# Short products held back into groups in a two-layer DeltaNet and attention trunk

## The chip, the cores and the metric

The kernel runs on one core of a Trainium2 chip. The metric is device time in microseconds (us) of one execution. The engines are TensorE (PE, with PEld for its weight loads), VectorE (DVE), ScalarE (ACT), GpSimd (POOL) and SyncE (SP), which issues the DMAs here. A line such as L137 is a line of the kernel before; the change adds lines, so that the same helper stands at L142 in the changed kernel.

## The reference, cut to what matters

Two layers over 1024 tokens of width 1024: a gated DeltaNet with chunked recurrence, then an attention with forget gates. Each is `x + gate * mixer(norm(x))`. The change concerns the first layer:

```python
def gated_delta_rule(q, k, v, g, beta):          # 16 value heads, head size 128
    ...
    L = jnp.where(strict, jnp.einsum('bhncd,bhnsd->bhncs', kb, k) * decay, 0.0)
    T = lax.linalg.triangular_solve(eye + L, ...)     # the inverse
    u = T @ vb
    w = T @ (kb * jnp.exp(g)[..., None])
    ...
    def step(state, inp):                             # the recurrence
        v_new = u_n - jnp.einsum('bhcd,bhde->bhce', w_n, state)
        o = (jnp.einsum('bhcd,bhde->bhce', q_n, state)
             + jnp.einsum('bhcs,bhse->bhce', a_n, v_new))
        state = state * gl_n[..., None, None] + jnp.einsum('bhcd,bhce->bhde', k_n, v_new)
        return state, o
```

Around it stand the input projection with a short causal convolution, and `o = rmsnorm(o, norm_w) * zg` followed by the output projection.

## The kernel before

The first layer is worked off in 16 iterations: two halves of 512 tokens, and in each half 8 groups of two value heads. The kernel uses chunks of 128 tokens, four in a half. Per iteration there are:

- the input projections (`proj_all`, `proj_tile`): long products with 512 columns, each weight and activation split in a high and a low part, so that three products stand for one (tiles `mm<-ht_h,whi`, `ht_l,whi`, `ht_h,wlo`). After the last iteration, `out_proj_a` adds the output projection of the first half (`mm<-whi,ohi` and its like) while the last recurrences still run, and later that of the second half, whose activations are loaded in pairs of heads (tiles `yh`, `yl`, L461);
- transposes and small products of preparation (`prepk`, `prepv`, `prep2`; tiles `tr`, `su`);
- the inverse of the triangular matrix, by blocks of 16, 32 and 64 (`invert_blocks` on VectorE and DMAs, `invert_merge` with products of 16, 32 and 64 columns; tiles `tmat`, `rmat`, `qq`, `pp`, `pq`);
- the recurrence (`chain`, L1033): per chunk `ch<-state,k` (the state read), VectorE's `xp` (L1050), `ch<-xp,rmat`, ScalarE's `vn` and VectorE's `ve`, `co<-vn`, `co<-ve`, VectorE's new `state` (L1095), and so on to the next chunk;
- `finish` (L1117): the output `og` is normalised, transposed (`tr<-ident,og`), gated, split in `ogh` and `ogl` (one buffer each) and stored to `og_d` and `ogl_d` (L1142), from which the output projection loads it again.

The long products are float32r, the short ones float32; a short product therefore shows as two records in the trace, a transpose as one.

The order of TensorE's instructions is written out by hand through a planner, the class `Flow`. Each of the streams above is a generator. `flow.t` is a plan clock that adds up the planned cost of each product. A generator yields a delay after which its next piece may be issued; `step` takes, among the streams that are due, the one with the lowest priority number. The long products are the stream with number 9, the fill; recurrence, inverse, preparation and finish have the numbers 1 to 6. So before the change a short piece is issued in the first step after it is due, and the fill takes what is left, three products at a time. Streams also hold on each other: `done["core"]` counts finished chains, and the projections of an iteration wait until an earlier chain is done. The order of the other engines and of SyncE's queue is made by the scheduler from this program, so a piece that moves takes its DMAs and vector instructions along.

Of the kernel before, what the change touches and what calls it, by code (L numbers as in the profile page):

```python
# [78 lines left out]
SC = 1.0  # L79
OGW = 2000  # L80
OL = 4
OX = 4
Y_NN = 8000
KPE = (7, 5)
KC = 3
# [26 lines left out]
class Flow:  # L112


    def __init__(self, tc):
        self.tc = tc
        self.nc = tc.nc
        self.t = 0.0
        self.n = 0
        self.live = []  # L120
        self.idle = 0.0
        self.rings = {}
        self.held = []
        self.kept = ()

    def _cost(self, lhs, rhs):
        n = rhs.free_size()
        if lhs.dtype == BF16:
            return max(0.42 * n, 29.0)
        m = lhs.free_size()  # L130
        if lhs.dtype == F32R:
            return max(0.42 * n, 107.0 * m / P)
        return max(1.67 * n, 214.0 * m / P)
# [43 lines left out]
            self.step()  # L177

    def step(self):
        for s in self.live:  # L180
            if s[3] <= self.t:
                with self.tc.high_priority(offset=s[4]):
                    d = next(s[2], None)
                if d is None:
                    self.live.remove(s)
                else:
                    s[3] = self.t + d * SC
                break
        else:
            t = min(s[3] for s in self.live)  # L190
            self.idle += t - self.t
            self.t = t
# [3 lines left out]
def tile_trunk(  # L196
# [26 lines left out]
    flow = Flow(tc)  # L223
# [127 lines left out]
    def hold(ok):  # L351
        while not ok():
            yield 300
# [90 lines left out]
    def out_o(k, tok):  # L444
        def load():
            w = 2 * P
            hi = xt_([P, w], "ohi", 4, F32R)
            lo = xt_([P, w], "olo", 4, F32R)
            for v, d in ((hi, og_d), (lo, ogl_d)):
                nc.sync.dma_start(v.bitcast(F32), d[k, :, tok : tok + w])  # L450
            return [(hi, lo)]

        return load
# [13 lines left out]
    def out_list(h):  # L467
        n = (512, D)[h]
        for tp in range(0, CPH, 2):
            for cs in range(0, D, n):  # L470
                w_src.extend(out_w(k, cs, n) for k in range(0, 16, D // n))
                if h:
                    k0 = 0 if tp else OX
                    o_src.extend(out_o(k, h * HALF + tp * P) for k in range(k0))
# [56 lines left out]
    with ExitStack() as sa:  # L531
# [3 lines left out]
        def at(shape, name, bufs=1, dt=F32):  # L535
            return pa.tile(shape, dt, name=name, tag=name, bufs=bufs)
# [128 lines left out]
        def norm_tile(xt, jk, evac, part=None):  # L665
# [4 lines left out]
            nc.vector.tensor_scalar(xt, xt, rs, None, op0=ALU.mult)  # L670
            yield Y_NN
            for k0 in range(0, KT, 4):
# [603 lines left out]
        def ada_all():  # L1276
            yield from hold(lambda: done["kp"] >= AD0 + 1)
            def al(shape, name, bufs):
                t = at([P, D], name, bufs) if name == "nx" else at([P, 512], name, bufs)
                return t[0 : shape[0], 0 : shape[1]]  # L1280

            for _ in range(2):
                nc.vector.tensor_copy(al([P, KT], "nx", 2), ts[AD0]["k"][:, 0, 0:KT])
            for l, cl in strips:
                yield from ada_strip(
                    al, acc_bank, l, cl, 512, ("nx", 2), ("nh", 2), ("nh", 2), 1, ADP
                )

        ts = []
        done = dict(kp=0, prep2=0, merge=0, kqv=0, tr=0, prep=0, chain=0, norm=0, start=0, inv=0, core=0, gates=0)  # L1290
# [11 lines left out]
        flow.add(prep2_all(), 4, HP)  # L1302
        flow.add(next_norm(), 5)
        flow.add(ada_all(), 6)
        flow.run(ch)
        while done["chain"] < 2 * NG:
            flow.step()
# [636 lines left out]
```

## Time and profile before

| | us |
|---|---|
| median of 3 runs | 1946.24 (1943.46 to 1947.99) |
| profiled execution | 1945.78 |
| its span, first to last instruction | 1943.8 |
| mean granted TensorE clock | 0.971 |

Stages by the trace: the start to about 165 us, iterations of the first layer to about 1051 us, the output projection's first half to about 1079 us and its second half from there to about 1200 us, then the second layer. The end of the third chain is near 321 us, that of the thirteenth near 884 us.

In the rows below, a timeline row has start and duration in us, then the engine, the line, the operation, the tiles (out<-in) and shapes and a count; in brackets the idle time of the engine before it and what ended that. A row of waits has total, times and longest, in us.

### The profile page before, as it was taken

The page shows a single profiled execution, that of the slowest core. Times are in us where ns is not written, and L with a number is a line of the kernel's source. Part 1 is how long each engine was busy: PE and PEld are TensorE (multiplying, and loading weights), DVE is VectorE, ACT ScalarE, POOL GpSimd, SP SyncE. Part 2 cuts the span into 40 slices and gives each one's busy share as a digit, 9 for nine tenths or more (in the row PEclk, how much of TensorE's full clock was granted, in tenths as well). Part 3 has the DMA queues.
Part 4 walks back from the last instruction along what each step waited for, and adds up shares of the span by engine and source line. Part 5 has one row for each costly group of instructions (what it writes and reads, how often), then busy time and mean ns, then how long its engine had stood idle before and what let it go on. Part 6 is the DMA issues. An engine that isn't in the chain of part 4 may idle for free.

```text
span 1943.8 us, 35877 instructions
## 1 busy us (share of the span) xinstructions
PE 1828.4 (94%) x12888; PEld 1524.4 (78%) x12888; DVE 1328.3 (68%) x3323; ACT 1033.3 (53%) x2674; POOL 367.0 (19%) x402
## 2 busy tenths in 40 slices
PE   6989999999899999999899799999999999999798
PEld 4767778777787878878776578798988988989576
DVE  5677888788786777776665585475665656656764
ACT  4565566565564555555444453465565555655631
POOL 1100110101210110010001244223223132221222
PEclk7889999899999999999999899999999999999899
DMA  7576767667656565454689982112021011112423
GB/s 270 187 229 205 233 210 245 207 212 249 229 181 186 173 192 176 148 172 138 206 268 320 356 303 98 31 48 66 24 65 60 23 60 45 44 55 71 155 87 95
DMA packets 224985, 307.16 MB, mean 158 GB/s; under 512 B 100460, under 2 KB 136940, under 8 KB 224808
## 3 DMA queue, kind: packets, MB, share of 16 engines
q1 hardware_dynamic: 223800, 304.65, 48.4%
q8 instruction: 101, 1.65, 0.4%
q14 instruction: 76, 0.62, 0.1%
q10 hardware_dynamic: 1008, 0.23, 0.1%
HBM read 223.15 MB, written 81.67 MB: 157 GB/s over the span
## 4 chain that ended last, share of the span: by engine, by line
PE 62%; DMA 14%; DVE 13%; ACT 4%; issue 3%; POOL 1%; SPq 1%; ACTq 0%; DVEq 0%; POOLq 0%
PE mm L137 39%; PE lg L137 5%; PE su L137 4%; PE pt L141 3%; PE oT L137 3%; DMA nx<-in_ada_w_dram 3%; PE tr L141 3%; PE ch L137 2%; DVE wlo L340 2%; PE co L137 2%; DVE cv_y L833 2%; DMA ohi<-og_d 2%; DMA rmat<-rb 1%; DMA wraw<-in_wb_dram 1%; ACT whi L337 1%
## 5 line engine op out<-in xcount | busy, mean ns | idle before, releaser
L137 PE MATMUL mm<-ht_h,whi 128*128 128x512 f32 x768 | 342.4, 446 | 0.5 <-DVE nh L313 0.5
L137 PE MATMUL mm<-ht_h,wlo 128*128 128x512 f32 x768 | 305.2, 397 | 0.0
L137 PE MATMUL mm<-ht_l,whi 128*128 128x512 f32 x768 | 304.3, 396 | 0.8 <-POOL ht_l L340 0.8
L137 PE MATMUL mm<-whi,h_h 128*128 128x384 f32 x512 | 186.7, 365 | 0.9 <-DVE kn L1533 0.9
L137 PE MATMUL mm<-wlo,h_h 128*128 128x384 f32 x512 | 172.6, 337 | 0.6 <-POOL wlo L340 0.6
L137 PEld LDWEIGHTS mm<-ht_h,wlo 128*128 128x128 f32 x768 | 146.3, 190 | 33.9
L137 PE MATMUL mm<-whi,h_l 128*128 128x384 f32 x512 | 172.7, 337 | 0.0
L1684 DVE TENSOR_TENSOR ptl<-pt,pth 128x512 fp32r<-128x512 f32 x192 | 106.4, 555 | 92.5 <-ACT pth L1683 90.5
L137 PEld LDWEIGHTS mm<-ht_h,whi 128*128 128x128 f32 x768 | 147.2, 192 | 28.4 <-issue 1.7
L137 PEld LDWEIGHTS mm<-ht_l,whi 128*128 128x128 f32 x768 | 147.7, 192 | 25.2 <-POOL ht_l L340 1.2
L1683 ACT CAST pth<-pt 128x512 fp32r<-128x512 f32 x192 | 91.3, 477 | 139.8 <-PE pt L141 139.0
L833 DVE SCALAR_TENSOR_TENSOR cv_y<-cv_t,conv_h,cv_y 128x512 f32<-128x512 f32 x192 | 144.4, 752 | 17.3 <-ACT cv_y L825 15.6
L1648 ACT ACTIVATE lg<-lg,mx 128x896 f32<-128x896 f32 (+7 forms) x128 | 99.5, 777 | 54.3 <-DVE mx L1640 48.6
L1527 POOL TENSOR_TENSOR rs<-ss,mhalf 128x4 f32<-128x4 f32 x64 | 64.5, 1007 | 330.8 <-DVE ss L1525 325.2
L340 DVE TENSOR_TENSOR wlo<-ht_h,whi 128x512 fp32r<-128x512 f32 x124 | 93.3, 792 | 47.3 <-ACT whi L337 45.1
L337 ACT CAST whi<-ht_h 128x512 fp32r<-128x512 f32 x124 | 70.7, 618 | 86.5 <-PE mm L137 38.6
L137 PE MATMUL mm<-h_h,whi 128*128 128x512 f32 x240 | 100.5, 419 | 0.7 <-DVE wlo L1783 0.3
L137 PEld LDWEIGHTS mm<-whi,h_h 128*128 128x128 f32 x512 | 97.8, 191 | 3.5 <-ACT v L1529 1.2
L137 PEld LDWEIGHTS mm<-wlo,h_h 128*128 128x128 f32 x512 | 97.2, 190 | 2.8 <-POOL wlo L340 0.8
L141 PE MATMUL pt<-ident,lg 128*128 128x128 f32 (+1 forms) x584 | 96.0, 273 | 3.1 <-ACT lg L1648 3.1
L137 PEld LDWEIGHTS mm<-whi,h_l 128*128 128x128 f32 x512 | 96.4, 188 | 0.0
L137 PE MATMUL mm<-h_h,wlo 128*128 128x512 f32 x240 | 94.9, 395 | 0.0
(390 smaller groups left out, 4492.9 us busy)
## 6 DMA issues: line engine op xcount, KB each, us to landing
ht_h<-in_wa_o_dram SPq DMA_DIRECT2D x62, 512.0 KB, 5.2
wc<-whi SPq DMA_DIRECT2D x45, 512.0 KB, 4.5
wc<-wlo SPq DMA_DIRECT2D x45, 512.0 KB, 4.3
wlo<-wc SPq DMA_DIRECT2D x45, 512.0 KB, 4.9
whi<-wc SPq DMA_DIRECT2D x45, 512.0 KB, 3.6
wlo<-in_wa_c_dram SPq DMA_DIRECT2D x35, 512.0 KB, 4.3
nx<-in_ada_w_dram SPq DMA_DIRECT2D x64, 256.0 KB, 3.4
wraw<-in_wb_dram SPq DMA_DIRECT2D x56, 256.0 KB, 2.8
```

The costliest lines, as they stand in the source:

```text
L137: self.nc.tensor.matmul(out, lhsT, rhs, start=start, stop=stop)
L141: self.nc.tensor.transpose(out, src, ident)
L337: nc.scalar.copy(hi, src)
L340: (lo_eng or nc.gpsimd).tensor_tensor(lo, src, hi.bitcast(F32), op=ALU.subtract)
L833: nc.vector.scalar_tensor_tensor(y, raw[:, j : j + HALF], w[:, j : j + 1], y, op0=ALU.mult, op1=ALU.add)
L1527: nc.gpsimd.tensor_tensor(rs, ss, mhalf[:, 0:4], op=ALU.pow)
L1648: nc.scalar.activation(lg, lg, AF.Exp, scale=-1.0, bias=mx[:, hh : hh + 1], accum_out=sums[:, tt : tt + 1],)
L1683: nc.scalar.copy(ph_[:, cs], pp[:, cs])
L1684: nc.vector.tensor_tensor(pl_[:, cs], pp[:, cs], ph_[:, cs].bitcast(F32), op=ALU.subtract)
```

## The change

The planner gets a gap. While `gap` is set, and no group of short pieces is open, short pieces that are due are skipped until `GAP` plan units (1000) have passed since the last short piece that issued a product, provided that the fill has something to issue. Once a short piece has issued a product, the group is open: other short pieces are then taken up to `PULL` (250) units before they are due. The group closes when the fill issues products. The next due time of a stream counts from the later of its due time and the clock. The gap is set when three chains are done and unset when thirteen are done; outside of that the rules are as before.

```diff
+GAP = 1000.0
+PULL = 250.0
...
     def step(self):
+        far = self.gap and not self.open and self.t - self.mark < self.gap and any(
+            s[0] == 9 and s[3] <= self.t for s in self.live
+        )
+        near = PULL if self.gap and self.open else 0.0
         for s in self.live:
-            if s[3] <= self.t:
+            if s[0] < 9 and far:
+                continue
+            if s[3] <= self.t + (near if s[0] < 9 else 0.0):
+                t0 = self.t
                 with self.tc.high_priority(offset=s[4]):
                     d = next(s[2], None)
                 if d is None:
                     self.live.remove(s)
                 else:
-                    s[3] = self.t + d * SC
+                    s[3] = max(self.t, s[3]) + d * SC
+                if s[0] == 9:
+                    if self.t > t0:
+                        self.open = False
+                elif self.t > t0:
+                    self.open = True
+                    self.mark = self.t
                 break
...
+        while done["core"] < 3:
+            flow.step()
+        flow.gap = GAP
+        while done["core"] < 13:
+            flow.step()
+        flow.gap = 0.0
         flow.run(ch)
```

No instruction is added or removed; TensorE, VectorE, ScalarE, GpSimd and SyncE have the same instructions in another order.

TensorE, in the tenth chain (second half, heads 2 and 3), from the state read to the step that needs it by way of VectorE. Before (each run of long products is shown by its first rows):

```order
L137 MATMUL ch<-state_142,k 128x256
L137 MATMUL mm<-ht_h,whi 128x512
L137 MATMUL mm<-ht_l,whi 128x512
L137 MATMUL mm<-ht_h,wlo 128x512
...
L141 MATMUL tr<-ident,og 128x128 x4
...
L137 MATMUL ch<-xp,rmat_131 128x128 x2
L137 MATMUL ch<-state_142,q 128x256
```

Now:

```order
L146 MATMUL tr<-ident,og 128x128 x4
L142 MATMUL ch<-state_142,k 128x256
L146 MATMUL tr<-ident,k 128x128 x4
L146 MATMUL tr<-ident,og 128x128 x4
L142 MATMUL ch<-xp,rmat_131 128x128 x2
L142 MATMUL ch<-state_142,q 128x256
L142 MATMUL su<-tmat_132,d_7987 32x16 x2
...
L142 MATMUL co<-vn,d_6855 128x128 x2
L142 MATMUL mm<-ht_h,whi 128x512
```

Twelve long products stood between `ch<-state,k` and `ch<-xp` before; now only transposes do, and the first piece of the next inverse follows in the same group.

TensorE, at the end of the first half's output projection, around the transposes of the last chain's output. Before:

```order
L137 MATMUL mm<-whi,olo 128x512
L141 MATMUL tr<-ident,og 128x128 x4
L137 MATMUL mm<-whi,ohi 128x512
L137 MATMUL mm<-wlo,ohi 128x512
...
L141 MATMUL tr<-ident,og 128x128 x4
L137 MATMUL mm<-whi,ohi 128x512
...
L137 MATMUL lg<-whi,ohi 128x512
```

Now:

```order
L142 MATMUL mm<-whi,olo 128x512
L146 MATMUL tr<-ident,og 128x128 x8
L142 MATMUL mm<-whi,ohi 128x512
L142 MATMUL mm<-wlo,ohi 128x512
L142 MATMUL mm<-whi,olo 128x512
L142 MATMUL lg<-whi,ohi 128x512
```

Before, 18 long products stood between the two heads' transposes and 12 more of the first half behind them; now both stand behind the last long product of the first half (`lg` is a bank that only the second half uses). In both orders 66 long products stand between the last `co<-ve` and the first of these transposes, so the last chain itself ends 30 long products later than before, counted from the end of that half.

SyncE's queue at the same place, from the last stores of `og_d` to the first load of `yh`. Before:

```order
L1142 DMA og_d<-ogh 128x512
L450 DMA olo<-ogl_d 128x256
L1142 DMA ogl_d<-ogl 128x512
L526 DMA x_d<-ht_l 128x1024
L433 DMA ht_h<-in_wa_o_dram 128x1024
...
L1372 DMA v<-x_d 128x1024
L343 DMA kn<-in_wb_dram 128x512
...
L461 DMA yh<-og_d 128x2x256
L461 DMA yl<-ogl_d 128x2x256
L507 DMA ht_l<-in_x_dram 128x1024
```

Now:

```order
L1160 DMA og_d<-ogh 128x512
L451 DMA ht_h<-in_wa_o_dram 128x1024
L544 DMA x_d<-ht_l 128x1024
L1160 DMA ogl_d<-ogl 128x512
L1160 DMA og_d<-ogh 128x512
L451 DMA ht_h<-in_wa_o_dram 128x1024
L525 DMA ht_l<-in_x_dram 128x1024 x3
L1160 DMA ogl_d<-ogl 128x512
L525 DMA ht_l<-in_x_dram 128x1024
...
L479 DMA yh<-og_d 128x2x256
L479 DMA yl<-ogl_d 128x2x256
```

The stores of both heads now follow each other behind the loads of the first half, and the four loads of `ht_l` (rows of x for the second half) moved ahead of the first `yh`.

More of the change, by code (lines that the diff above doesn't have):

```diff
@@ L124, in __init__ @@
         self.kept = ()
+        self.gap = 0.0
+        self.open = False
+        self.mark = 0.0
     def _cost(self, lhs, rhs):
@@ L186, in step @@
                 else:
-                    s[3] = self.t + d * SC
+                    s[3] = max(self.t, s[3]) + d * SC
+                if s[0] == 9:
+                    if self.t > t0:
+                        self.open = False
+                elif self.t > t0:
+                    self.open = True
+                    self.mark = self.t
                 break
```

## The prediction

> **What bounds the kernel now.** I read the page first, then a table by stretches, then TensorE's waits in the stretch that the change rewrites, then single rows of the timeline.
>
> ```profile
> PE 1828.4 (94%) x12888; PEld 1524.4 (78%) x12888; DVE 1328.3 (68%) x3323; ACT 1033.3 (53%) x2674; POOL 367.0 (19%) x402
> PE 62%; DMA 14%; DVE 13%; ACT 4%; issue 3%; POOL 1%; SPq 1%; ACTq 0%; DVEq 0%; POOLq 0%
> ```
>
> The first row is busy time by engine, the second the chain that ended last. TensorE is busy 94% of the span and carries 62% of the chain. Its products stay the same in number and shape, so the time can change only where TensorE waits, or at a seam between long and short products.
>
> ```profile
> 321.00:884.00 563.00, 539.03 (x4824) 437.86 (x4822) 435.23 (x1150) 315.81 (x963) 66.28 (x95) 0.98 0.62 196
> 1051.00:1080.00 29.00, 26.12 (x111) 19.31 (x111) 18.24 (x29) 12.14 (x24) 6.13 (x5) 1.00 0.92 306
> 1080.00:1110.00 30.00, 19.02 (x77) 14.93 (x75) 13.97 (x30) 11.18 (x23) 4.68 (x5) 0.83 1.02 387
> 1110.00:1270.00 160.00, 153.54 (x760) 126.18 (x761) 104.03 (x230) 72.42 (x147) 65.34 (x52) 0.98 0.44 150
> ```
>
> Columns are length, then busy time of PE, PEld, DVE, ACT and POOL, the granted clock, the DMA share and GB/s. Chains 4 to 13, which the new rule covers, run from about 321 to 884 us. There TensorE is idle for 563 - 539.03 = 24 us; that is all that better placing of short products could win in the stretch. The second place is the seam between the two layers, 1080 to 1110 us: TensorE is idle 11 us of 30, and the DMA engines are full (1.02).
>
> ```profile
> PE tr L141 <- ACT rmat L1218: 5.7, 3, 3.0
> PE su L137 <- DVE tmat L1223: 3.6, 4, 2.2
> PE ch L137 <- DVE state L1095: 2.7, 4, 1.2
> PE ch L137 <- DVE xp L1050: 1.1, 2, 0.7
> ```
>
> These are the waits of 321 to 884 us (total, times, longest). They are many small ones, of the inverse (rmat, tmat) and of the recurrence (state, xp), not one repeated stall.
>
> **The change part by part.**
>
> *Seams.* In the order, long products of the first layer's projections are parted by 292 groups of short ones before and 271 now; 20 of the 21 lost are in the rewritten stretch (193, now 173).
>
> ```profile
> 705.99 0.39 PE L137 MATMUL mm<-ht_l,whi 128*128 128x512 f32 x1
> 706.22 0.39 PE L137 MATMUL mm<-ht_h,wlo 128*128 128x512 f32 x1
> 706.45 0.60 PE L137 MATMUL co<-vn,d 128*128 128x128 f32 x4
> 706.89 0.60 PE L141 MATMUL tr<-ident,vt 128*128 128x128 f32 x4
> 707.25 0.48 PE L137 MATMUL mm<-ht_h,whi 128*128 128x512 f32 x1
> 707.57 0.40 PE L137 MATMUL mm<-ht_l,whi 128*128 128x512 f32 x1
> ```
>
> A long product takes a step of 706.22 - 705.99 = 0.23 us; the four records of two float32 products take 0.44 (706.89 - 706.45). From the first short to the second long after them are 1.12 us, and 0.44 + 0.44 + 0.23 = 1.11: a seam costs 0.01 us. 21 fewer save 0.2 us. Bounds: nothing, and 21 times the 0.09 by which the first long product's step is over 0.23 (707.57 - 707.25 = 0.32), 1.9 us. I take 0.2, since the whole group's sum includes that step.
>
> The Trainium skill, "TensorE: Matmul & The Clock Gate", section "Single matmul latency", speaks for the change here: a warm product whose fill and drain are not overlapped lasts (398 + N)/2.4 ns instead of about N/2.4. If each seam exposed that, it would be an estimated 0.17 us each and 3.5 us in all, and the sum would be some 3 us lower. The rows above do not agree: the float32 and the long products overlap across the seam.
>
> *Waits of the rewritten stretch.* The rule moves short steps in both directions: held back until 1000 of the planner's units have passed, and taken up to 250 early once a group is open. What counts is the work between a step and the one that needs its result.
>
> ```profile
> 900.15 0.59 PE L137 MATMUL ch<-state,k 128*128 128x256 f32 x2
> 900.78 0.61 DVE L1050 SCALAR_TENSOR_TENSOR xp<-ch,g_neg,vtok 128x128 f32<-128x128 f32 x2 [1.15 <-PE ch L137]
> 698.85 0.67 PE L137 MATMUL ch<-state,k 128*128 128x256 f32 x2
> 702.94 0.71 PE L137 MATMUL ch<-xp,rmat 128*128 128x128 f32 x4 [0.47 <-DVE xp L1050]
> ```
>
> At best the input of the next step is ready 900.78 + 0.61 - 900.15 = 1.24 us after the product started. With other work ahead on VectorE it was 4.09 us (702.94 - 698.85). Before, the rows of the tenth chain shown with the change had twelve long products and four transposes between the two steps: 12 x 0.23 + 0.44, and 0.44 for the first step itself (two records of twice the width), 3.6 us. Now eight transposes stand there: 0.88 + 0.44 = 1.3 us, just enough at best and 2.8 short at worst. Pricing every gap between consecutive chain steps of the stretch in this way, one place has under 1.75 us of work before, and six have now. Behind the waiting product stand all of TensorE's later rows, so a wait there is paid in full. Five more such places at 0 to 2.8 us are 0 to 14 us; against that, other waits of the 24 us vanish, because held steps come later after their inputs. I take the lower part, 0.6 us a place, **+3 us**, since most inputs come nearer 1.24 than 4.09. The bounds of this term are -12 (half of the 24 us gone) and +12.
>
> *The seam between the layers.* The gap rule ends at chain 13, but what it pushed back is not made good: in the new order the last chain ends 30 long products later, and the transposes of its output (finish, `og`) stand behind all of the first half's output projection instead of within it.
>
> ```profile
> 1069.00 0.60 PE L141 MATMUL tr<-ident,og 128*128 128x128 f32 x4
> 1073.70 0.60 PE L141 MATMUL tr<-ident,og 128*128 128x128 f32 x4
> 1077.84 0.40 PE L137 MATMUL mm<-whi,olo 128*128 128x512 f32 x1
> 1099.33 0.76 PE L137 MATMUL mm<-whi,yh 128*128 128x512 f32 x1 [9.59 <-DMA yh<-og_d]
> 1110.13 0.50 PE L137 MATMUL mm<-whi,yl 128*128 128x512 f32 x1 [1.52 <-DMA yl<-ogl_d]
> ```
>
> ```profile
> 1077.60 0.62 ACT L337 CAST ogh<-ogt 128x512 fp32r<-128x512 f32 x1 [2.53 <-DMA og_d<-ogh]
> ```
>
> ```profile
> 1071.82 0.32 SPq L1142 DMA_DIRECT2D og_d<-ogh  x1
> 1090.83 0.33 SPq L1427 DMA_DIRECT2D qk_c<-in_qkn_dram  x1
> 1092.07 0.33 SPq L1430 DMA_DIRECT2D fb<-in_f_bias_dram  x1
> 1093.35 0.38 SPq L461 DMA_DIRECT2D yh<-og_d  x1
> ```
>
> Before, the first head's transposes start at 1069.00, its store `og_d` is issued at 1071.82, 2.82 us later, and the second head's `ogh`, which has one buffer, waits for that store until 1077.60, 5.78 us after the issue. The 4.7 us between the two transposes covered part of that store. Now both start only behind the last long product of that half: 1077.84 + 0.23 = 1078.07. Then the first store goes out at 1080.9, the second `ogh` can be written at 1086.7, **9.1 us later** than 1077.60. SyncE's queue is in order: the second store stands ahead of the loads of `v`, `kn` and `yh` there, so `yh`, issued 15.75 us after that `ogh` (1093.35 - 1077.60), moves with it, and TensorE, which already waits 9.59 us for `yh`, waits about 18.7. The order shows TensorE no other work ahead of it than before: the products of the second half's first four heads.
>
> Besides, four loads of `ht_l` now stand ahead of `yh`, not behind. At the queue's pace there (1092.07 - 1090.83 = 1.24 us) they would add up to 5 us, less where the queue has emptied while it waited for the store; I take 1. In return the 1.52 us for `yl` should go. The term is 9.1 + 1.0 - 1.5, **+8.6 us**.
>
> ```profile
> og_d<-ogh SPq DMA_DIRECT2D x32, 256.0 KB, 3.5
> ```
>
> Bounds: with the median landing of such a store, 3.5 us instead of 5.78, the shift is 6.8; if the loads before `yh` also close up in a queue that has emptied, +3; with all of the `ht_l` loads in the way, 9.1 + 5 = +14. The stage behind has no slack to give back (153.54 us busy of 160).
>
> The Trainium skill, "DMA: Bandwidth & Descriptors", section "Anatomy of one DMA — SWDGE (gpsimd) path", would make this smaller: its fit of 2.0 us plus bytes over 436 GB/s gives an estimated 2.6 us for such a store, and by it the shift would be 5.9 instead of 9.1 us and the forecast some 3 us lower. The store here took 5.78 on full DMA engines, and goes by that row.
>
> **Sum.** The profiled execution took 1945.78 us (span 1943.8, 2.0 around it), 0.46 under the median of the runs shown. 1945.78 - 0.2 + 3 + 8.6 = 1957.2, so **1957 us**, 0.55% slower.
>
> **Rivals.**
> - *The held steps find their inputs ready (faster).* Place: chains 4 to 13. A short product that waits in the plan for its group lets VectorE and ScalarE finish, and half of the 24 us of idle time goes. For it: the waits there are short (at most 3.0 us), so a delay of the size of the gap covers them. Against it: steps taken early, and six thin places where one was. With the tail at +4: 1945.8 - 0.2 - 12 + 4 = 1938. It decides as soon as the stretch wins more than the seam between the layers loses, some 9 us. Chance 0.2.
> - *Nothing to be seen.* 20 fewer groups at 0.01 us are nothing, the waits move about without a balance, and the store's delay hides behind loads of `v` and `kn` that full DMA engines hold back anyway. For it: the DMA share of 1.02. The tail's +3 then meets -3 in the stretch: 1946. Chance 0.2.
> - *The forecast, and worse.* The layer seam alone, +8.6, with the stretch between 0 and +12: 1954 to 1966, at most 1971 with the tail's upper bound. Chance 0.6.
>
> **How the numbers follow.** The likeliest case gives 1957, with 1950 to 1968 as its own range. To leave no more than 2 in 10 out, the range reaches down to the faster rival, 1938, and up to 1970, where both terms are near their upper bounds. A measurement of this kernel can tell about 0.2% (4 us) from no change. Faster by over 0.2%: 0.2. Within it: 0.2. Slower by over 0.2%: 0.6.
>
> **What would show it.** In the profile of the changed kernel: the row of the first `yh` product should have about 18 us of idle time before it, and the two `tr<-ident,og` rows of the last chain should stand together. The long step stays 0.23 us and a seam 0.01. TensorE's idle time in the stretch from the third chain to the thirteenth should be about 27 us; under 15 would make the forecast wrong by itself, and so would a first `yh` at the same distance from the last `og` store with the store on time. A last chain that ends as early as before would take away the larger term.

## The result, and the profile after

The changed kernel takes 1968.53 us (median of 4 runs, 1964.87 to 1973.83), the kernel before 1945.05 (4 runs, 1943.46 to 1947.99). The ratio is 1.0107, with a 95% interval of 1.0081 to 1.0133: 1.07% slower, about 21 us (16 to 26). The profiled execution took 1971.17 us, with a span of 1969.2.

First the busy time by engine of the changed kernel:

```profile
PE 1833.2 (93%) x12888; PEld 1526.9 (78%) x12888; DVE 1325.5 (67%) x3323; ACT 1031.5 (52%) x2674; POOL 369.5 (19%) x402
```

The same instructions keep TensorE busy 4.8 us longer (1833.2 against 1828.4), while the span grows by 25.4. Most of the difference is therefore TensorE waiting. Where it waits is shown by a table of stretches (length, busy time of PE, PEld, DVE, ACT, POOL, granted clock, DMA share, GB/s), the first row for chains 4 to 13, the other two at the seam between the layers:

```profile
321.00:898.00 577.00, 546.27 (x4856) 443.78 (x4854) 436.38 (x1152) 317.13 (x968) 67.76 (x96) 0.98 0.60 192
1070.00:1098.00 28.00, 23.11 (x104) 17.72 (x103) 16.84 (x27) 10.43 (x22) 4.62 (x3) 1.00 0.96 322
1098.00:1128.00 30.00, 15.79 (x54) 12.35 (x53) 7.21 (x14) 7.65 (x15) 3.04 (x3) 0.67 0.94 352
```

In chains 4 to 13 TensorE now idles 577 - 546.27 = 30.7 us (24 before). The seam between the layers has grown too: in the 30 us around the first `yh` product TensorE is busy 15.79 us where it was busy 19.02, at a clock of 0.67 where it was 0.83.

To compare stretches that hold the same work in every kernel, I cut at products and not at chain ends. The "stretch" runs from the 721st long product of the projections, just behind the third chain, to the last one; the "seam part" runs from there to the last `yh` product. The same table for before (first two rows) and for the changed kernel:

```profile
326.70:946.20 619.50, 595.53 (x5317) 484.75 (x5317) 475.30 (x1260) 344.97 (x1052) 69.70 (x97) 0.98 0.59 187
946.20:1191.80 245.60, 220.36 (x1180) 174.28 (x1179) 156.12 (x282) 112.08 (x244) 52.71 (x36) 0.95 0.87 297
```

```profile
329.70:961.90 632.20, 598.18 (x5307) 486.09 (x5307) 473.07 (x1257) 342.66 (x1048) 69.92 (x97) 0.98 0.58 183
961.90:1217.00 255.10, 222.23 (x1190) 175.23 (x1189) 155.90 (x284) 112.69 (x248) 53.74 (x36) 0.94 0.83 286
```

The stretch is 632.2 - 619.5 = 12.7 us longer, the seam part 255.1 - 245.6 = 9.5. The rest is 3 us ahead of the stretch, where the order of TensorE is the same in both, and so is no effect of it; behind the last `yh` product both kernels take 752 us. In the stretch the idle time grew from 24.0 to 34.0 us. The time at half clock (worked out from the trace's clock records, since two digits are too coarse) grew from 20.5 to 27.3 us. About half of it is lost: a long product's step is 0.43 us there (median) and 0.23 at full clock. So 10.0 + 3.4 = 13.4, near the 12.7.

The waits of TensorE in that stretch, after (total, times, longest):

```profile
PE ch L142 <- DVE state L1113: 4.8, 6, 1.5
PE ch L142 <- DVE xp L1068: 4.4, 5, 1.9
PE tr L142 <- ACT sqt L1007: 2.9, 1, 2.9
PE tr L146 <- ACT rmat L1236: 2.9, 2, 2.7
PE tr L146 <- DVE vt L858: 2.6, 1, 2.6
PE su L142 <- ACT qq L1224: 2.1, 1, 2.1
...
PE tr L146 <- ACT vtok L1028: 1.9, 1, 1.9
PE su L142 <- DVE d L993: 1.8, 1, 1.8
PE ch L142 <- ACT cv_t L855: 1.8, 1, 1.8
```

I group such rows by what the wait ended with: the recurrence (`state`, `xp`, `vn`, `ve`), the inverse (`tmat`, `rmat`, `qq`, `pp`, `pq`, `xi`, and the `d` that is written at the inverse's end), or the preparation (`vt`, `k`, `sqt`, `ktok`, `vtok`, `cv_t`, `cv_y`, and `d` of L993; the convolution behind the projections writes `vt`, `k`, `cv_t` and `cv_y`). Recurrence 6.6 before and 10.7 now; inverse 10.8 and 7.4; preparation 2.8 and 11.3; the rest 3.4 and 4.2. The largest growth, 8.5 us, is in waits for the preparation. These are sums of one execution each.

The place of the tenth chain that the prediction spoke of, on TensorE and on VectorE, with three stretches around it (columns as above):

```profile
692.09 0.67 PE L142 MATMUL ch<-state,k 128*128 128x256 f32 x2 [0.39 <-DVE state L1113]
692.60 0.60 PE L146 MATMUL tr<-ident,k 128*128 128x128 f32 x4
693.60 0.66 PE L146 MATMUL tr<-ident,og 128*128 128x128 f32 x4 [0.40 <-DVE ogt L1151]
695.44 0.71 PE L142 MATMUL ch<-xp,rmat 128*128 128x128 f32 x4 [1.19 <-DVE xp L1068]
...
698.20 0.20 PE L142 MATMUL tr<-tmat,d 16*32 16x16 f32 x1 [1.44 <-DVE ogt L1151]
```

```profile
693.46 0.74 DVE L304 SCALAR_TENSOR_TENSOR nh<-nx,cond,nh 128x512 f32<-128x512 f32 x1
694.12 0.74 DVE L851 SCALAR_TENSOR_TENSOR cv_y<-cv_t,conv_h,cv_y 128x512 f32<-128x512 f32 x1
694.78 0.60 DVE L1068 SCALAR_TENSOR_TENSOR xp<-ch,g_neg,vtok 128x128 f32<-128x128 f32 x2
```

```profile
690.00:697.00 7.00, 4.78 (x32) 3.30 (x30) 6.98 (x16) 5.12 (x19) 0.09 (x1) 1.00 0.78 253
695.30:698.71 3.41, 1.83 (x70) 1.41 (x70) 2.83 (x6) 1.08 (x3) 1.44 (x1) 1.00 1.01 360
698.71:702.12 3.41, 3.41 (x29) 2.89 (x17) 3.16 (x8) 2.77 (x8) 0.00 (x0) 0.50 0.56 177
```

Three streams that each need VectorE stand in one group: the recurrence, the finish and the inverse. VectorE is busy 6.98 of 7.00 us and works off its queue; `xp` is made behind one instruction that sums over the weights `ada_w` (`nh`) and one of the projections' convolution (`cv_y`). So it is not the streams of the group alone that queue there. Four waits follow each other, and then the clock drops to half (0.50 from 698.71 on).

The seam between the layers, on TensorE and then on ScalarE and SyncE:

```profile
1091.72 1.03 PE L146 MATMUL tr<-ident,og 128*128 128x128 f32 x8
1097.14 0.47 PE L142 MATMUL lg<-whi,ohi 128*128 128x512 f32 x1 [3.68 <-DVE ogt L1151]
1123.43 0.77 PE L142 MATMUL mm<-whi,yh 128*128 128x512 f32 x1 [14.21 <-DMA yh<-og_d]
```

```profile
1099.82 0.62 ACT L355 CAST ogh<-ogt 128x512 fp32r<-128x512 f32 x1 [5.90 <-DMA og_d<-ogh]
```

```profile
1093.95 0.60 SPq L1160 DMA_DIRECT2D og_d<-ogh  x1
1116.76 0.38 SPq L479 DMA_DIRECT2D yh<-og_d  x1
```

Both heads' transposes stand together (the count is 8). The first store is issued at 1093.95 and the second `ogh` written 5.87 us later; `yh` is issued 16.94 us behind that, and its product waits 14.21 us.

### The profile page after: what moved, and what is told of

Its sections match the earlier page's. It is cut to its first block, busy times and chain, and to the rows that moved or that the text cites. A ratio compares the mean times of both kernels' runs of the same rounds, so it can differ in the third digit from the quotient of the medians.

```text
span 1969.2 us, 35866 instructions
## 1 busy us (share of the span) xinstructions
PE 1833.2 (93%) x12888; PEld 1526.9 (78%) x12888; DVE 1325.5 (67%) x3323; ACT 1031.5 (52%) x2674; POOL 369.5 (19%) x402
## 4 chain that ended last, share of the span: by engine, by line
PE 61%; DMA 15%; DVE 13%; ACT 4%; issue 3%; SPq 2%; POOL 1%; ACTq 0%; DVEq 0%; POOLq 0%
PE mm L142 38%; PE lg L142 5%; PE su L142 4%; PE pt L146 3%; PE oT L142 3%; DMA nx<-in_ada_w_dram 3%; PE ch L142 3%; PE tr L146 2%; DVE wlo L358 2%; PE co L142 2%; DVE cv_y L851 1%; DMA wraw<-in_wb_dram 1%; DMA ht_h<-in_wa_o_dram 1%; DMA lb<-d 1%; ACT whi L355 1%
```

## The experiments

All comparisons are ratios to runs of the kernel before that were made beside them, on the same chip. The median of those runs was 1942.24 us for the first four experiments, 1948.78 for the next four (from `shift_p2`) and 1948.51 for the last four; microseconds below are the ratio less one, times that median. Theories A, B and C belong to the first four experiments, T, D and P to the next four; in the last four T and P go on, and C is a new theory. In the table, "seam" is the seam part of the profiled execution less the 245.6 us of before, "rest" is the whole less the seam, "idle" and "half" are TensorE's idle time and the time at half clock in the stretch (24.0 and 20.5 us before). The seam, idle and half columns come from one execution each.

```
kernel          ratio   interval           whole   seam   rest   idle   half
(the change)    1.0107  1.0081 to 1.0133   +20.8   +9.5   +11.3  34.0   27.3
early_finish    1.0069  1.0043 to 1.0096   +13.4   -0.9   +14.3  33.8   27.3
gap_3_8         1.0086  1.0063 to 1.0109   +16.7   +2.9   +13.8  30.6   34.1
pull_100        1.0120  1.0089 to 1.0151   +23.4   +6.8   +16.6  35.4   44.4
pull_only       1.0093  1.0070 to 1.0115   +18.1   +2.9   +15.2  37.2   27.3
pull_500        1.0061  1.0041 to 1.0082   +11.9   -5.0   +16.9  35.9   30.7

late_finish     1.0060  1.0039 to 1.0080   +11.7   +9.4    +2.3  28.7   20.5
gap_8_13        1.0068  1.0041 to 1.0094   +13.2   +9.7    +3.5  30.7   17.1
shift_p2        1.0015  0.9998 to 1.0031    +2.9   +0.1    +2.8  27.2   23.9
shift_c1        1.0067  1.0048 to 1.0087   +13.1   +9.0    +4.1  27.0   23.9
hold_only       1.0072  1.0044 to 1.0100   +14.0  +10.3    +3.7  26.0   20.5
hold_early      1.0022  1.0004 to 1.0040    +4.3   +0.2    +4.1  27.1   17.1
hold_2000       1.0259  1.0218 to 1.0299   +50.5   +6.1   +44.4  51.0   54.6
```

How much one execution can say is seen where two kernels have the same order in the stretch. `late_finish` has the order of before there, yet its idle time is 28.7 and its stretch 5.1 us longer. The change and `early_finish`, and `hold_only` and `hold_early`, agree within 1.2 us of stretch and 1.1 of idle time.

### The seam between the layers

`late_finish` is the kernel before with the finish of the last chain alone put off; `early_finish` is the changed kernel with it brought forward.

```diff
-            yield Y_F0 - 3000
+            yield Y_F0 - 3000 + (6000 if (h, g) == (1, NG - 1) else 0)     # late_finish
+            yield Y_F0 - 3000 + (-6000 if (h, g) == (1, NG - 1) else 0)    # early_finish
```

> The kernel before, with one change: the finish of the last chain is due 6000 plan units later, so that both heads' transposes stand behind the last long product of the first half's output projection, as in the changed kernel; everything up to there is in the old order. Theory A (two separate terms, the layer seam is worth what the trace shows between the end of the projections and the first yh product, 8.4 us): slower than before by 8 us, 1953, with 13 to 15 us of idle time before the first yh product. Rival B (all of the loss is made in chains 4 to 13, and the later yh only hides or shifts what would be lost anyway): within 2 us of before.

> The changed kernel, with one change: the finish of the last chain is due 6000 plan units earlier, so that its transposes stand 24 and 6 long products ahead of the end of that half again. Theory A: 8 us come back, 1960 to 1961, and the idle time before the first yh product is near 10 us. Against A: if the transposes now wait for VectorE's scaling of og, a part of this is lost again, 1964. Rival B: no change, 1968.

The rows of `late_finish`, then of `early_finish`:

```profile
1084.23 1.03 PE L141 MATMUL tr<-ident,og 128*128 128x128 f32 x8
1116.33 0.77 PE L137 MATMUL mm<-whi,yh 128*128 128x512 f32 x1 [13.72 <-DMA yh<-og_d]
```

```profile
1081.74 0.60 PE L146 MATMUL tr<-ident,og 128*128 128x128 f32 x4
1087.43 0.60 PE L146 MATMUL tr<-ident,og 128*128 128x128 f32 x4
1110.68 0.77 PE L142 MATMUL mm<-whi,yh 128*128 128x512 f32 x1 [9.61 <-DMA yh<-og_d]
```

With nothing but the transposes moved behind the end of the half, the kernel before gets 11.7 us slower (7.6 to 15.5), 9.4 of them in the seam part. With the transposes apart again in the changed kernel, the wait is 9.61 us as before (9.59), and the seam part loses nothing. This term is shown in both directions, and rival B, by which nothing would change, falls. What `early_finish` keeps, +13.4, is the stretch.

### Where in the stretch the rule does harm

```diff
-        while done["core"] < 13:
+        while done["core"] < 8:      # gap_3_8: the rule for chains 4 to 8 alone
```

```diff
-        while done["core"] < 3:
+        while done["core"] < 8:      # gap_8_13: the rule for chains 9 to 13 alone
```

> The gap rule from the third to the eighth chain only. In the changed kernel's trace the lead over before, taken at equal numbers of long products and less the short work done, went from +3.0 us after chain 3 to -3.4 us at about 545 us (chain 7), so this half of the rule looked like a gain there. Theory A (the loss sits in the later half, where held steps leave places with too little between them): the stretch is 0 to 5 us faster than before, and what the last chain's finish does at the layer seam is added (its transposes stand 18 and 0 long products ahead of the end here, +4): 1942 to 1949. Rival C (the rule costs alike everywhere): 1953 to 1957.

> The gap rule from the eighth to the thirteenth chain only. Theory A: most of the stretch's loss, 13 to 20 us, and the layer seam's 8 us (both transposes behind the end): 1966 to 1973. Rival C (costs alike everywhere): half of the stretch's 15.7 us and the seam's 8 us: 1961.

The theory that the loss sits in the late chains (A) missed both, and so did rival C, by which the rule costs alike everywhere. The rule in chains 9 to 13 alone costs 3.5 us besides the seam, the rule in chains 4 to 8 alone 13.8, as much as all of it. Yet in the trace of `gap_3_8` the loss comes after the rule has ended: up to the 1393rd long product it is 8 us ahead of before, and from there to the last one it takes 363.4 us where before took 341.8. So what the rule does early is paid later as well.

The losses of the kernels do not lie in one place. I cut the stretch into pieces of 144 long products (one iteration each) and add up idle time and half of the time at half clock in each. Against before, the change loses most in four pieces: 4.4 us between the 1297th and the 1441st long product, then 3.1, 6.0 and 5.0 us in three pieces behind the 1584th. `gap_3_8` loses 12.1 us between the 1585th and the 1729th. The three kernels that only take early (below) lose 6.7 to 13.6 us between the 1297th and the 1441st alone. `hold_early` loses 7.0 there too and `hold_only`, in the same order, 1.3, so a single piece is uncertain by several us.

### Another order, or this rule?

`shift_p2` and `shift_c1` are the kernel before without the rule, with one planned delay changed by 100 or 50 units; the order then differs from the fourth or fifth chain on. `hold_only` and `pull_only` are the two halves of the rule: holding back until the gap has passed, and taking early once a group is open.

```diff
-Y_P2 = 3000
+Y_P2 = 3100      # shift_p2 (the kernel before)
-Y_C1 = 2200
+Y_C1 = 2250      # shift_c1 (the kernel before)
-PULL = 250.0
+PULL = 0.0       # hold_only (the changed kernel)
-GAP = 1000.0
+GAP = 1.0        # pull_only (the changed kernel)
```

> The kernel before, without the new rule; one delay of the preparation (Y_P2) is 3100 units and not 3000. From the fourth chain on the short steps fall in other places, as under the change, but nothing is held or taken early. Short groups: 297 (292 before, 271 with the change). Chain steps with under 1.5 us of work ahead of the one that needs them, in the stretch of chains 4 to 13: two (one before, eight with the change). The transposes of the last output stand with 18 long products between them and none behind, which in the last call cost about 3 us. Theory T (thin places cost the time): stretch within 3 us of before, total about 1947. Theory D (any other order costs it, because the delays fit the old one): stretch 10 us longer, total about 1956, with TensorE's waits in chains 9 to 11 up by more than 5 us.

> The kernel before, without the new rule; one delay of the recurrence (Y_C1) is 2250 units and not 2200, so that the order moves from the fifth chain on. 293 groups; three places with under 1.5 us of work. Both transposes of the last output stand behind the last long product of the first half, as with the change. All theories: first yh product waits 13 to 15 us, +9.4 us at the seam between the layers. Theory T: stretch +1 to +3, total about 1954. Theory D: stretch +10, total about 1962.

> The changed kernel with PULL at 0: short steps are held until the gap has passed, but none is taken early. 274 groups; six places with under 1.5 us of work; both transposes of the last output behind the end of the first half (+9.4 at the seam). Theory T: stretch +8 to +10, total about 1961. Theory D: the same. Rival P (the loss comes from steps taken before they are due, and holding is harmless): stretch +0 to +2, total about 1953.

> The changed kernel with GAP at 1 unit: nothing is held, but once a group is open short steps are taken up to 250 units early. 276 groups; three places with under 1.5 us of work, none in front of the product that waits for xp. The last chain ends earlier than before (18 long products between the transposes and 24 behind, 12 before), so nothing is lost at the seam between the layers, and up to 2 us may be won. Theory T: stretch +0 to +3, total 1942 to 1946. Theory D: stretch +10, total about 1953. Rival P: stretch +10 or more, total about 1954.

The two orders without the rule, and the one that only holds, lose 2.8 to 4.1 us besides the seam. `late_finish`, whose order in the stretch is that of before, shows 2.3 by the same sum, so these are hardly to be told from nothing. Theory D, that any other order costs 10 us, falls. `hold_only`, at 3.7, lies between P (0 to 2) and T (8 to 10), nearer to P. `pull_only` loses 15.2 us; theory T, by which its three thin places should have cost 3 us at most, fails here, and rival P holds. At the seam `pull_only` was to lose nothing and lost 2.9 us.

TensorE's longest waits in the stretch, of `hold_only` and then of `pull_only`:

```profile
PE ch L142 <- DVE state L1113: 8.7, 6, 2.6
PE tr L146 <- ACT vtok L1028: 3.8, 2, 2.4
PE su L142 <- DVE tmat L1266: 2.1, 2, 1.2
PE co L142 <- DVE ve L1088: 2.1, 2, 1.4
```

```profile
PE su L142 <- DVE tmat L1212: 6.4, 2, 6.2
PE ch L142 <- DVE state L1113: 5.1, 5, 1.9
PE tr L146 <- DVE vt L858: 4.7, 2, 3.2
PE tr L142 <- ACT ktok L1011: 3.3, 3, 1.7
PE su L142 <- DVE d L1047: 2.9, 1, 2.9
```

Holding trades one kind of wait for another: the recurrence 12.6 us (6.6 before), the inverse 5.5 (10.8 before), and 25.8 in all. Taking early adds waits for the inverse (16.1) and for the preparation (8.3; 2.8 before). Over all kernels of the table the waits for the inverse and the preparation together are 17.7 to 24.4 us where steps are taken early in chains 4 to 8, and 9.1 to 16.4 where they are not (`hold_2000` apart). The two groups are no further apart than one execution from another (13.5 before, 16.4 in `late_finish` with the same order), and `shift_p2` has 10.0 us of waits for the preparation, nearly as much as the change, and loses almost nothing. The lost time as a whole tells them apart better: idle time and half of the half-clock time, from the table, are together 13 to 23 us above before in the six kernels of the upper part, and 1 to 5 in the first six of the lower part.

How the inverse gets late is seen on VectorE, in the loop that inverts the 16x16 blocks of the ninth inverse. First and last row of that loop, before, and then in `pull_only`:

```profile
552.50 0.17 DVE L1167 TENSOR_TENSOR xtmp<-lr,xi 128x15 f32<-128x15 f32 x1
...
575.98 0.17 DVE L1171 TENSOR_TENSOR xi<-xi,xtmp 128x8 f32<-128x8 f32 x1
```

```profile
556.87 0.17 DVE L1185 TENSOR_TENSOR xtmp<-lr,xi 128x15 f32<-128x15 f32 x1 [2.42 <-DMA lr<-lb]
...
587.94 0.16 DVE L1189 TENSOR_TENSOR xi<-xi,xtmp 128x8 f32<-128x8 f32 x1
```

It lasted 23.5 us before and lasts 31.1 now: 36 other VectorE instructions came between its 30, now 59. Behind it, SyncE stores the blocks and loads them again, and the merge on TensorE waits 6.2 us for them. In the six kernels of the upper part of the table this loop lasts 26.0 to 31.6 us with 48 to 59 other instructions in it, in the first six of the lower part 19.3 to 25.9 us with 30 to 37. A long loop does not make the wait by itself: in the change it lasts 29.0 us, and the merge behind it waits 0.2 us. In the three kernels that only take early the loop also ends later, 259 to 262 us behind the start of the stretch, against 255 in the change and 249 before. So the late ninth inverse accounts for a part of what those three lose, and not for the loss of the change.

### How much is held, and how much is taken early

```diff
-PULL = 250.0
+PULL = 0.0       # hold_early, with the finish 6000 units earlier as in early_finish
-GAP = 1000.0
-PULL = 250.0
+GAP = 1.0
+PULL = 100.0     # pull_100
+PULL = 500.0     # pull_500
-GAP = 1000.0
-PULL = 250.0
+GAP = 2000.0
+PULL = 0.0       # hold_2000
```

> The changed kernel with PULL at 0 (short steps are held, none is taken early) and the transposes of the last output 6000 units earlier, so that 18 long products stand between the two heads and 12 behind them, as before the change. Theory P (the loss of the stretch comes from steps taken early; holding trades waits within groups for waits at their start): seam between the layers +0, stretch +2 to +4, ratio about 1.0015. Theory T (places with little work between two chain steps cost the time; six here): ratio 1.005. Theory C (every new order loses 3 us, and some lose 10 more at one place by accident): the order up to the last chain is that of hold_only, so 1.0015 too.

> The changed kernel with GAP at 1 (nothing is held) and PULL at 100 instead of 250. 18 long products between the last transposes, none behind (+3 at most at the seam, by the trace of shift_p2 +0). Theory P: waits behind the first product of a group, 17.7 us before and 31.4 with PULL 250, about 23; stretch +5 to +8, ratio 1.003 to 1.005. Theory C: no order by PULL; either +3 or +13, whichever falls, and where it is +13 one place with a wait of over 2.5 us and a window of half clock makes most of it.

> As pull_100, with PULL at 500. 18 long products between the last transposes and 6 behind (+0 to +2 at the seam). Theory P: waits behind the first product of a group above the 31.4 us of PULL 250, about 40; stretch +20 or more, ratio 1.010 or more. Theory C: not above PULL 250 by rule; +3 or +13.

> The changed kernel with PULL at 0 and GAP at 2000: 220 groups (271 with the change, 292 before), and 17 places with under 1.5 us of work between two chain steps (eight with the change). Transposes of the last output both behind the end (+9.5). Theory P: waits within groups not above before's 17.7 us, stretch +3 to +6, ratio 1.007. Theory T: 16 more thin places at about 1 us each, stretch +15 to +20, ratio 1.013 to 1.015. Rival seam (fewer groups win): 72 fewer groups at 0.01 us are 0.7 us, nothing to be seen.

The size that theory P gave was wrong: 100, 250 and 500 units cost 16.6, 15.2 and 16.9 us besides the seam. What goes with the loss is that steps are taken early at all in chains 4 to 8, not by how much. Theory C, by which an order loses 3 or 13 us by accident, fits the values but hardly their sorting: the six kernels that take early in chains 4 to 8 are all at 11 to 17 us, six that do not all at 2 to 4. This sorting was made after the results, with `gap_8_13`, which takes early in later chains, in the second group; and as some kernels share an order, there are four different orders of chains 4 to 8 on each side. So C is made unlikely, not excluded. The seam part of `pull_100` came out at +6.8 us where 3 at most were expected, that of `pull_500` at -5.0 where 0 to 2 were. Waits of `pull_100` and `pull_500`:

```profile
PE tr L146 <- DVE k L858: 6.0, 1, 6.0
PE su L142 <- DVE tmat L1212: 5.6, 2, 5.4
```

```profile
PE su L142 <- DVE tmat L1212: 5.0, 2, 4.8
```

All three kernels that only take early wait for the same `tmat`, 5.0 to 6.4 us. `hold_early` keeps the grouping (274 groups, 292 before) without its two costs, and is 4.3 us slower than before (0.8 to 7.8); its first `yh` product waits 7.75 us. Set beside `early_finish`, from which it differs in `PULL` alone, it is the cleanest test of taking early: 1.0022 (1.0004 to 1.0040) against 1.0069 (1.0043 to 1.0096). It beats the change, not the kernel before, and no kernel here did.

`hold_2000` went past both forecasts, at 50 us, with 6.1 at the seam where 9.5 were expected. Its waits:

```profile
PE su L142 <- DVE tmat L1212: 10.4, 2, 10.1
PE co L142 <- DVE ve L1088: 10.0, 5, 3.7
PE su L142 <- DVE tmat L1241: 5.1, 7, 1.5
PE su L142 <- DVE tmat L1266: 4.0, 1, 4.0
```

With 220 groups TensorE idles 27 us more and spends 34 us more at half clock: 27 + 17 = 44, its rest. Holding is not harmless at that size. The recurrence has 16.5 us of waits, where before had 6.6; but `hold_only` and `hold_early`, with fewer thin places, have 12.6 and 14.7 and lose little, so the thin places are not shown to be the cause. The largest wait, 10.1 us, is again for the inverse, which has nearly 25 us in all.

## Why the prediction came out as it did

The sign was right, and so was the mechanism of the larger term. The size was about half: 11 us slower were forecast and about 21 measured, and 1968.53 lies 1.5 us under the upper end of the range, 1970.

*Seams, -0.2.* Not contradicted, and too small to be measured. The long step stays 0.23 us. The order with 72 groups fewer is the slowest of all, and nothing was won by fewer groups anywhere. The estimate of 3.5 us after the Trainium skill, "TensorE: Matmul & The Clock Gate", section "Single matmul latency", finds no support in these runs. That section gives the time of a single bf16 product; the products here are float32r and float32.

*The seam between the layers, +8.6.* Right in mechanism, and 9.5 in the trace. The steps repeat: the second `ogh` comes 5.87 us after the first store's issue (the row of before, used as the price, said 5.78), and `yh` is issued 16.94 us after that `ogh` (15.75 + 1.0 in the sum). Taken from the last projection, the second `ogh` is 6.5 us later, from there to the first `yh` product are 1.9 more, and 1.1 up to the last; the forecast had 9.1, 1.0 and -1.5. The transposes start 2.0 us sooner after the last projection than the forecast had them. The 1.52 us for `yl` went, as forecast, but waits for `wlo` came in its place. So the parts are each off by 1 to 2.6 us, and that they add up to nearly the forecast sum is in part luck. The wait itself was given as about 18.7 us and is 14.21, since 3.68 us now fall ahead of it, at `lg`, which waits for `ogt`. By the estimate of 2.6 us from "DMA: Bandwidth & Descriptors" of the Trainium skill (section "Anatomy of one DMA — SWDGE (gpsimd) path") the term would have been 5.4. That section is about DMAs that GpSimd issues, and SyncE issues this store; the measured 5.87 decides for the row.

*Waits of the rewritten stretch, +3.* This term was mis-sized: 11.3 by the whole, 12.7 in the trace, where its upper bound was 12. Its step was "0.6 us a place", for places with little work between two steps of the recurrence. For what it priced it was near: the waits of the recurrence grew by 4.1 us, and the tenth chain's `ch<-xp` waits 1.19. (How many thin places there are is not settled: the prediction counts six under 1.75 us, the expectations eight under 1.5.) What it left out is twice as large. The rule takes steps of the preparation early as well, and no cover was priced for them: waits for the preparation grew by 8.5 us, and by 7.9 in `early_finish`, while the hoped-for gain, in the inverse, was 3.4. And it had no price for the clock. Its premise that the time can change only where TensorE waits, or at a seam, left that out: 6.8 us more at half speed are 3.4 lost here, and the seam part has 30.7 us at half clock where it had 23.9. The runs without early steps in chains 4 to 8 lose 2 to 4 us in its place. So the sum's +3 would have been near for a rule that only holds, at this gap; at a gap of 2000 units holding alone cost 44.

*The signs.* TensorE's idle time in chains 4 to 13 was to be 27 us and is 30.7. For the rival by which held steps find their inputs ready only the waits of the inverse speak (10.8 us before, 7.4 now, 5.5 in `hold_only`). `late_finish`, with the order of before, has 14.0 and `shift_p2`, which holds nothing, 6.2, so a part of that is scatter or comes with any new order.

*Left open.* Which chain of events makes the loss of the change itself: the two halves of the rule are told apart, but the places where the change loses are not those of the kernels that only take early. Why 100 units of early taking, less than half the planned cost of one long product (215 units), cost as much as 500. The rows show what goes with it (VectorE's order, the late ninth inverse, the waits for `k` and `vt`), not why any small advance brings it about. Nor is it shown why taking early in chains 9 to 13 alone does no such harm. Waits are read from one execution each; the five of `late_finish` ran from 1953.68 to 1963.77 us with one order, and the slowest is the one that was profiled.

## What to carry to other kernels

Before short products are packed into groups, count what else they share: in a group without long products TensorE leaves VectorE no time, and the steps of the group queue there, here behind instructions of other streams as well. Price all streams that a rule moves, not only the longest dependent chain, and each wait with the clock it costs. And a rule that ends somewhere still shifts what comes after it; look at the next stage's first load, as here, where 30 long products of delay cost 9.5 us of the 21.

## What was not expected of the hardware

The clock fell to half without any long pause. In the tenth chain the longest wait is 1.44 us and TensorE is busy 1.83 of 3.41 us, yet a window of 3.4 us at half clock follows (the 0.50 above). The same was seen in the stretch of all traces, with windows of 3.4 us and multiples; in the kernel before, the three of the stretch come behind 3.41 us in which TensorE was busy 1.2 to 1.6 us and never idle for longer than 2.22. In the Trainium skill, "TensorE: Matmul & The Clock Gate" has the clock fall after an idle window of about 3.4 us (section "Part 1: The HAM clock gate (the "warmup" mystery)"), but also tells of short pauses between groups of products that are enough (section "A second HAM failure mode: psum-queue depth-cycling"). The length of the first and the short pauses of the second agree with these runs; a wholly idle window was not needed. The cost adds up: from before to `hold_2000` the idle time of the stretch rises by 27 us and the time at half clock by 34.
